# Prompt attention taken two heads at a time, each head on its own half of the TensorE array

## The chip, the cores and the metric

The kernel is one program on one core of one Trainium2 chip. The metric is the device time of one execution in microseconds (us). Before the change three timed runs gave 1269.4, 1271.23 and 1272.8 us: a median of 1271.23 us. One further execution was profiled; that one took 1273.75 us, of which the profile covers a span of 1272.0 us.

Engines are named as the profile names them: PE is the matrix engine (TensorE), PEld its weight loads, DVE VectorE, ACT ScalarE, POOL GpSimd, SP the engine that issues most DMAs.

## The reference, cut to what matters

One inference step of a decoder layer on 256 prompt rows and 32 sample rows: normalise, one wide input projection, a short convolution branch, an attention branch, gates and an output projection, then a retrieval layer (PEER). The change touches the prompt's attention alone. It has three groups of 8 heads of width 64, each group with its own window and dilation; the softmaxes of the three groups of a head are joined.

```python
N_SLOTS, HEAD_DIM, Q_BLOCK = 8, 64, 128
GROUPS = ((128, 1), (512, 4), (2048, 16))
def _dilated_group(q, k_ext, v_ext, ...):          # one group, all 8 heads
    s = einsum('bthd,btkhd->bthk', q, kg)
    s = s * (HEAD_DIM ** -0.5) - slopes[:, None] * dist[None, :]
    s = where(valid, s, -inf)
    m = max(s); p = exp(s - m); l = sum(p)
    o = einsum('bthk,btkhd->bthd', p, vg) / l
    lse = m + log(l)
def _combine(outs, lses):                          # over the three groups
    w = softmax(stack(lses, axis=0), axis=0)
    return sum(w[..., None] * stack(outs, axis=0), axis=0)
```

Because the groups of a head are joined by their denominators, the kernel takes one softmax over the scores of the three groups side by side, and adds the three groups' values into one output.

## The kernel before, in words

**Weights stream past the whole kernel.** 368 blocks of 128 x 1024 floats are loaded in a fixed order (`load_to`, four raw buffers), and each is split into two fp32r halves: ACT makes `whi` (L102), DVE or POOL `wlo` (L103), up to three blocks ahead. A projection block is 8 times 3 matmuls (`mm3`, L118 to L120) into one of two PSUM banks called `acc`. The order of the blocks is: 12 for q, 12 for k, 12 for v, 24 for the convolution, 16 for its output and gate A, 12 for attention's output and gate B, 8 for W_o, 16 for PEER's queries, 128 + 128 for its experts.

**Everything else of attention is threaded between these blocks.** Each piece of attention is a Python generator in a list (`Flow`). `flow.step()` is called at the start and in the middle of most projection blocks; it lets each generator in the list emit its next piece of instructions. A generator may hand back a condition (free PSUM banks, free buffers), and then waits whole steps until it holds. There are six PSUM banks called `bg` for this work. So the order of instructions on every engine is fixed when the program is built: a piece of attention that PE has to do stands between two projection matmuls, and PE takes its queue in order.

**Prompt attention before** (`attn_prompt(t, s)`): t is a tile of 128 queries (0 or 1; keys are 128 (t+1)), s one of 8 heads. 16 generators, in turn:

- scores (L307): for each of three groups a matmul with 64 rows of contraction (the head's 64 channels, in rows 0 to 63 for an even head and 64 to 127 for an odd one), 128 query columns and 128 or 256 keys. Every fp32 matmul is two PE instructions, so a head has 6 on PE;
- bias and mask on DVE (L312, for tile 1 also L315), the softmax (`softmax`, L286 to L292: maximum and scale on DVE, a step; exp on ACT, a step; reciprocal and multiply on DVE, a step);
- transposes of the probabilities on PE (L328), 3 for tile 0, 6 for tile 1, into banks of four; ACT copies them to SBUF (L332);
- values (L338): 3 or 6 matmuls with 128 rows and 64 columns of stationary data (V of the head), accumulated in 64 partitions of one bank: 6 or 12 PE instructions;
- DVE copies the 64 x 128 result to `oT` (L342).

**Sample attention** runs through the same list: scores at L372 and L381, values at L426 and L434, transposes at L408 and L444. Its matmuls have 32 columns of stationary data, and four of them in a row go to four column groups of the array. Each of its 28 chunks of keys or values is loaded by POOL's queue when a buffer comes free.

What follows attention is `split_o`, which needs all heads, and the first block that reads its result stands at block 76. `flow.drain()` ahead of that block empties the list.

Of the kernel before, what the change touches and what calls it, by code (L numbers as in the profile page):

```python
# [10 lines left out]
F32 = mybir.dt.float32  # L11
# [5 lines left out]
OP = mybir.AluOpType  # L17
AX = mybir.AxisListType

P = 128  # L20
D = 1024
NT = 288
# [4 lines left out]
HD = 64  # L27
# [39 lines left out]
def emit(ctx, tc, a):  # L67
# [127 lines left out]
    if True:  # L195
        with ExitStack() as c1:
# [44 lines left out]
            sc_t = Banks(wk, "sc", 3)  # L241
            pt_t = Banks(wk, "pt", 2)
# [52 lines left out]
            def attn_prompt(t, s):  # L295
                pr, hf = divmod(s, 2)
                rows = slice(64 * hf, 64 * hf + 64)
# [4 lines left out]
                yield lambda: bg.free >= (nk if vdone[0] else nk + 1) and sc_t.free >= 1  # L302
                sc_t.free -= 1
                pb = [bg.get() for _ in range(nk)]
# [5 lines left out]
                sc = wk.tile([P, 1024], F32, tag="sc", name=f"sc{t}_{s}", bufs=sc_t.n)  # L310
                n1 = n if t == 0 else 512
                V.scalar_tensor_tensor(sc[:, :n1], biasP[:, off:off + n1], -8.0 * SLOPES[s], pb[0][:, :n1],  # L312
                                       op0=OP.mult, op1=OP.add)
                if t:
                    V.scalar_tensor_tensor(sc[:, 512:768], biasP[:, off + 512:off + 768], -8.0 * SLOPES[s],  # L315
                                           pb[1][:, :256], op0=OP.mult, op1=OP.add)
                bg.put(nk, later=True)
                yield from softmax(sc, n, f"pp{t}_{s}")
                yield lambda: bg.free >= nk and pt_t.free >= 1 and vdone[0]
                pt_t.free -= 1  # L320
                pt = wk.tile([P, 8, P], F32, tag="pt", name=f"pt{t}_{s}", bufs=pt_t.n)
                tbs = []
                for j0 in range(0, nb, 4):
                    j1 = min(nb, j0 + 4)
                    tb = bg.get()
                    tbs.append((tb, j0, j1))
                    for j in range(j0, j1):
                        T.transpose(tb[:, (j - j0) * P:(j - j0 + 1) * P], sc[:, j * P:(j + 1) * P], ident)  # L328
                sc_t.put(1, later=True)
                yield  # L330
                for tb, j0, j1 in tbs:
                    S.copy(pt[:, j0:j1, :].rearrange("p a b -> p (a b)"), tb[:, :(j1 - j0) * P])  # L332
                    bg.put(1, later=True)
                yield lambda: bg.free >= 1 and vdone[0]
                o = bg.get()
                for j in range(nb):
                    g, kb = divmod(j, nk)
                    T.matmul(o[rows, :P], vn[:, kb, g * 512 + s * HD:g * 512 + (s + 1) * HD], pt[:, j, :],  # L338
                             start=j == 0, stop=j == nb - 1)
                pt_t.put(1, later=True)  # L340
                yield
# [956 lines left out]
```

## Time and profile before

| what | value |
|---|---|
| median of 3 timed runs | 1271.23 us |
| the profiled execution | 1273.75 us |
| its span in the profile | 1272.0 us |
| PE busy over the span | 1233.2 us, 97% |
| DVE / ACT / POOL busy | 938.8 / 592.4 / 147.2 us |
| mean granted TensorE clock | 0.991 |
| prompt attention on PE, first to last instruction | 105 to 316 us of the span |

A row of the page's fifth part names a line, an engine, an operation, the tiles written and read, how often it ran, its busy time with the mean of one, and the idle time before it with what ended it. The PE durations are those of single instructions that overlap: two matmuls that start 0.13 us apart are each shown with 0.3 us. So what a stretch of PE work costs is read from starts, that is from the distance between the projection matmul ahead of it and the one behind it, and not from the sum of durations. The chain of waits shows stretches in this way: each piece lasts until the next begins.

### The profile page before, as it was taken

The page shows a single profiled execution, that of the slowest core. Times are in us where ns is not written, and L with a number is a line of the kernel's source. Part 1 is how long each engine was busy: PE and PEld are TensorE (multiplying, and loading weights), DVE is VectorE, ACT ScalarE, POOL GpSimd, SP SyncE. Part 2 cuts the span into 40 slices and gives each one's busy share as a digit, 9 for nine tenths or more (in the row PEclk, how much of TensorE's full clock was granted, in tenths as well). Part 3 has the DMA queues.
Part 4 walks back from the last instruction along what each step waited for, and adds up shares of the span by engine and source line. Part 5 has one row for each costly group of instructions (what it writes and reads, how often), then busy time and mean ns, then how long its engine had stood idle before and what let it go on. Part 6 is the DMA issues. An engine that isn't in the chain of part 4 may idle for free.

```text
span 1272.0 us, 23011 instructions
## 1 busy us (share of the span) xinstructions
PE 1233.2 (97%) x9140; PEld 1129.3 (89%) x9140; DVE 938.8 (74%) x1732; ACT 592.4 (47%) x978; POOL 147.2 (12%) x107
## 2 busy tenths in 40 slices
PE   9999999999998899999999999999999999999996
PEld 9898998888998899989999999999888888888884
DVE  6836376764555566998997898999677777777875
ACT  5334443333353455534554444444455555555553
POOL 1000000000000033444400000000111111111100
PEclk9999999999998899999999999999999999999998
DMA  8687666666458667768677777666778888888872
GB/s 326 223 292 262 239 236 224 214 233 224 146 166 282 234 235 274 273 241 287 243 257 263 286 260 280 248 225 219 273 256 301 305 308 297 309 303 296 311 253 102
DMA packets 67900, 324.49 MB, mean 255 GB/s; under 512 B 8512, under 2 KB 8672, under 8 KB 58832
## 3 DMA queue, kind: packets, MB, share of 16 engines
q1 hardware_dynamic: 55984, 249.46, 56.1%
q0 software_dynamic: 9600, 67.19, 14.1%
q10 hardware_dynamic: 2208, 6.37, 1.3%
q8 instruction: 72, 1.18, 0.4%
q14 instruction: 36, 0.29, 0.1%
HBM read 317.01 MB, written 60.10 MB: 296 GB/s over the span
## 4 chain that ended last, share of the span: by engine, by line
PE 86%; DVE 7%; ACT 2%; DMA 2%; issue 2%; SPq 1%; DVEq 0%; ACTq 0%
PE wide L1080 26%; PE acc L118 17%; PE acc L119 16%; PE acc L120 16%; PE wide L1000 2%; DVE wlo L103 2%; DMA raw<-wpack 2%; PE bg L338 1%; ACT whi L102 1%; PE bg L307 1%; PE bg L426 1%; PE bg L372 1%; DVE tp_eq L851 1%; PE bg L328 1%; DVE qbd L358 1%
## 5 line engine op out<-in xcount | busy, mean ns | idle before, releaser
L103 DVE TENSOR_TENSOR wlo<-raw,whi 128x1024 fp32r<-128x1024 f32 x338 | 417.5, 1236 | 243.0 <-ACT whi L102 240.9
L102 ACT CAST whi<-raw 128x1024 fp32r<-128x1024 f32 x368 | 386.3, 1050 | 181.6 <-PE wide L1080 158.5
L118 PE MATMUL acc<-h2H,whi 128*128 128x256 f32 x1024 | 292.4, 286 | 0.0
L120 PE MATMUL acc<-h2H,wlo 128*128 128x256 f32 x1024 | 287.7, 281 | 4.3 <-DVE wlo L103 4.0
L119 PE MATMUL acc<-h2L,whi 128*128 128x256 f32 x1024 | 289.5, 283 | 0.0
L1080 PE MATMUL wide<-whi,aa 128*128 128x512 f32 x1008 | 270.0, 389 | 1.6 <-ACT aa L1067 1.6
L1080 PEld LDWEIGHTS wide<-whi,aa 128*128 128x128 f32 x1008 | 189.1, 188 | 41.8 <-ACT aa L1067 2.7
L120 PEld LDWEIGHTS acc<-h2H,wlo 128*128 128x128 f32 x1024 | 192.5, 188 | 4.9 <-DVE wlo L103 4.5
L118 PEld LDWEIGHTS acc<-h2H,whi 128*128 128x128 f32 x1024 | 194.0, 190 | 0.2 <-issue 0.2
L119 PEld LDWEIGHTS acc<-h2L,whi 128*128 128x128 f32 x1024 | 193.6, 189 | 0.0
L118 PE MATMUL acc<-hH,whi 128*128 128x288 f32 x512 | 157.3, 307 | 1.8 <-ACT hH L478 1.1
L1080 PE MATMUL wide<-wlo,aa 128*128 128x512 f32 x504 | 155.1, 389 | 0.0
L120 PE MATMUL acc<-hH,wlo 128*128 128x288 f32 x512 | 150.7, 294 | 1.5 <-DVE wlo L103 1.5
L119 PE MATMUL acc<-hL,whi 128*128 128x288 f32 x512 | 151.2, 295 | 0.4 <-DVE hL L480 0.4
L1080 PEld LDWEIGHTS wide<-wlo,aa 128*128 128x128 f32 x504 | 94.6, 188 | 19.6
L118 PEld LDWEIGHTS acc<-hH,whi 128*128 128x128 f32 x512 | 96.0, 188 | 13.5 <-issue 8.5
L120 PEld LDWEIGHTS acc<-hH,wlo 128*128 128x128 f32 x512 | 96.3, 188 | 1.8 <-DVE wlo L103 1.8
L119 PEld LDWEIGHTS acc<-hL,whi 128*128 128x128 f32 x512 | 96.2, 188 | 0.6 <-DVE hL L480 0.6
L103 POOL TENSOR_TENSOR wlo<-raw,whi 128x1024 fp32r<-128x1024 f32 x30 | 76.1, 2537 | 130.8 <-ACT whi L102 123.4
L952 ACT ACTIVATE act<-acc 128x256 f32<-128x256 f32 (+30 forms) x124 | 40.8, 329 | 95.2 <-PE acc L120 94.9
L1091 POOL DMA_INDIRECT gt<-uv,eidx x32 | 48.6, 1517 | 271.0 <-DVE accS L1100 258.1
L949 ACT ACTIVATE hots<-acc 128x256 f32<-128x256 f32 (+31 forms) x65 | 18.5, 284 | 121.1 <-issue 115.7
(319 smaller groups left out, 1669.4 us busy)
## 6 DMA issues: line engine op xcount, KB each, us to landing
raw<-wpack SPq DMA_DIRECT2D x368, 512.0 KB, 3.8
kvs<-cache SPq DMA_DIRECT2D x32, 1020.0 KB, 6.9
kvs<-cache SPq DMA_DIRECT2D x16, 1016.0 KB, 7.3
kv<-kc POOLq DMA_DIRECT2D x14, 1024.0 KB, 6.8
kv<-vc POOLq DMA_DIRECT2D x14, 1024.0 KB, 6.0
kvs<-cache SPq DMA_DIRECT2D x8, 496.0 KB, 4.8
kT_out<-kT ACTq DMA_DIRECT2D x1, 1728.0 KB
v_out<-vn ACTq DMA_DIRECT2D x6, 256.0 KB, 5.5
```

What stands on the lines that cost most here:

```text
L102: S.copy(hi, raw)
L103: (G if i in pool_lo else V).tensor_sub(lo, raw, hi.bitcast(F32))
L118: T.matmul(out, wh, xh, start=first, stop=False)
L119: T.matmul(out, wh, xl, start=False, stop=False)
L120: T.matmul(out, wl, xh, start=False, stop=last)
L307: T.matmul(dst, qT[rows, g * 4 + pr, t * P:(t + 1) * P], kT[rows, g * 4 + pr, 0:w], start=True, stop=True)
L328: T.transpose(tb[:, (j - j0) * P:(j - j0 + 1) * P], sc[:, j * P:(j + 1) * P], ident)
L949: S.activation(e[:, :g], o[:, :g], AF.Gelu)
L952: S.activation(dst[:, g:], o[:, g:NP], AF.Gelu)
L1000: T.matmul(full[:, jj * P:(jj + 1) * P], e[:, 1, j // 2, :, j % 2], w[:, i, j // 2, :, j % 2], start=i == 0, stop=i == 1)
L1080: T.matmul(vacc[t][:, nn], x[:, tt], w[:, nn], start=i == 0 and j == 0, stop=i == 127 and j == 2)
L1091: G.indirect_dma_start(out=gt, out_offset=None, in_=a["uv"], in_offset=bass.IndirectOffsetOnAxis(ap=eidx[:, j:j + 1], axis=0))
```

## The change

`attn_prompt(t, pr)` now takes a pair of heads, 2 pr and 2 pr + 1. There are 8 generators in place of 16.

- Scores: for each group one matmul of the even head (rows 0 to 63) and one of the odd head (rows 64 to 127) by turns, each head into a bank of its own. For tile 1 the first two groups are one step, the third a later one, with two more banks.
- The softmaxes of both heads go side by side in the same steps.
- Transposes come three at a time for each head: one round for tile 0, two rounds for tile 1. After each round and its copies on ACT come the value matmuls of those three blocks, the two heads by turns, into partitions 0 to 63 and 64 to 127 of one bank.
- One DVE copy of 128 x 128 moves both heads' result.
- Four score buffers of 992 columns in place of three of 1024, and four steps in place of two between the starts of generators.

The number of matmuls, transposes, copies on ACT and bias operations stays the same; the copies to `oT` are 8 in place of 16.

```diff
-            sc_t = Banks(wk, "sc", 3)
+            sc_t = Banks(wk, "sc", 4)
...
-            def attn_prompt(t, s):
+            def attn_prompt(t, pr):
+                heads = (2 * pr, 2 * pr + 1)
+                rows = (slice(0, 64), slice(64, 128))
...
-                for g in range(3):
-                    dst = pb[0][:, g * w:(g + 1) * w] if t == 0 or g < 2 else pb[1][:, :w]
-                    T.matmul(dst, qT[rows, g * 4 + pr, t * P:(t + 1) * P], kT[rows, g * 4 + pr, 0:w],
-                             start=True, stop=True)
+                for gs in (range(3),) if t == 0 else (range(2), range(2, 3)):
+                    if gs.start:
+                        yield lambda: bg.free >= (2 if vdone[0] else 3)
+                    pb = [bg.get() for _ in range(2)]
+                    for g in gs:
+                        for h in range(2):
+                            T.matmul(pb[h][:, (g - gs.start) * w:(g - gs.start + 1) * w],
+                                     qT[rows[h], g * 4 + pr, t * P:(t + 1) * P], kT[rows[h], g * 4 + pr, 0:w],
+                                     start=True, stop=True)
+                    yield
...
+                sm = [softmax(scs[h], n, f"pp{t}_{heads[h]}") for h in range(2)]
+                while True:
+                    if [next(x, 1) for x in sm] == [1, 1]:
+                        break
+                    yield
...
+                for j0 in range(0, nb, 3):
...
+                    for h in range(2):
+                        tb = bg.get()
+                        tbs.append(tb)
+                        for j in range(3):
+                            T.transpose(tb[:, j * P:(j + 1) * P], scs[h][:, (j0 + j) * P:(j0 + j + 1) * P], ident)
...
+                    yield
+                    for h in range(2):
+                        S.copy(pt[:, 4 * h:4 * h + 3, :].rearrange("p a b -> p (a b)"), tbs[h][:, :3 * P])
+                    bg.put(2, later=True)
+                    yield
+                    for j in range(j0, j0 + 3):
+                        g, kb = divmod(j, nk)
+                        for h in range(2):
+                            T.matmul(o[rows[h], :P], vn[:, kb, g * 512 + heads[h] * HD:g * 512 + (heads[h] + 1) * HD],
+                                     pt[:, 4 * h + j - j0, :], start=j == 0, stop=j == nb - 1)
...
-                V.tensor_copy(oT[rows, pr, t * P:(t + 1) * P], o[rows, :P])
-                punits[0] += 1
+                V.tensor_copy(oT[:, pr, t * P:(t + 1) * P], o[:, :P])
+                punits[0] += 2
```

The built programs show what this does to the order. On PE, around the convolution's last blocks, before: the values of head 2 (L338) and the scores of head 5 (L307) of tile 1 stand in one gap between projection matmuls (L118 to L120).

```order
L338 MATMUL bg71_3151<-pt1_2_3102,vn_91 64x128 x6
L307 MATMUL bg72_3165<-kT_90,qT_89 128x256 x2
L307 MATMUL bg73_3166<-kT_90,qT_89 128x256
L118 MATMUL acc56_3176<-hH_81,whi58_3032 128x288
L119 MATMUL acc56_3176<-hL_209,whi58_3032 128x288
L120 MATMUL acc56_3176<-hH_81,wlo58_3033 128x288
```

The same place in the changed program, where the scores are L311, the transposes L335 and the values L348: the scores of heads 4 and 5 alternate between two banks (bg65, bg66), and their third group comes in a later gap, next to the second round of transposes of heads 2 and 3 (sc1_2, sc1_3).

```order
L120 MATMUL acc56_3118<-hH_81,wlo58_3001 128x288
L311 MATMUL bg65_3178<-kT_90,qT_89 128x256
L311 MATMUL bg66_3179<-kT_90,qT_89 128x256
L311 MATMUL bg65_3178<-kT_90,qT_89 128x256
L311 MATMUL bg66_3179<-kT_90,qT_89 128x256
L118 MATMUL acc57_3190<-hH_81,whi59_3064 128x288
...
L335 MATMUL bg67_3239<-ident_70,sc1_2_2776 128x128 x3
L335 MATMUL bg68_3243<-ident_70,sc1_3_2777 128x128 x3
L311 MATMUL bg69_3247<-kT_90,qT_89 128x256
L311 MATMUL bg70_3248<-kT_90,qT_89 128x256
L118 MATMUL acc58_3257<-zH_1825,whi60_3112 128x288
```

What moved: 3 + 3 score matmuls of two heads in two gaps became 4 + 2 in two gaps, each by turns over the two row halves. In all, prompt attention stands on PE in 36 places in place of 48 (12 of transposes, 12 of values, 12 of scores, where before there were 16 of each); some of these share a gap with each other or with sample attention. The last values of the prompt stand in block 67, before in block 64 or 65; the sample's last work stands in block 69 as before.

On DVE, the softmax of heads 4 and 5 of tile 1 before: each head's bias (L312, L315), maximum (L286) and scale (L287) are a run of their own, with a weight split (L103) between the heads.

```order
L312 SCALAR_TENSOR_TENSOR sc1_4_3158<-bias_77,bg69_3132 128x512
L315 SCALAR_TENSOR_TENSOR sc1_4_3158<-bias_77,bg70_3133 128x256
L286 TENSOR_REDUCE pp1_4_m_3161<-sc1_4_3158 128x1
L287 TENSOR_SCALAR pp1_4_m_3161<-pp1_4_m_3161 128x1
L103 TENSOR_TENSOR wlo60_3171<-raw60_2942,whi60_3170 128x1024
L342 COPY oT_93<-bg71_3151 64x128
L312 SCALAR_TENSOR_TENSOR sc1_5_3206<-bias_77,bg72_3165 128x512
L315 SCALAR_TENSOR_TENSOR sc1_5_3206<-bias_77,bg73_3166 128x256
L286 TENSOR_REDUCE pp1_5_m_3209<-sc1_5_3206 128x1
L287 TENSOR_SCALAR pp1_5_m_3209<-pp1_5_m_3209 128x1
```

In the changed program (bias is L317, the copy to `oT` L352) both heads' operations stand together:

```order
L317 SCALAR_TENSOR_TENSOR sc1_4_3176<-bias_77,bg69_3247 128x256
L317 SCALAR_TENSOR_TENSOR sc1_5_3177<-bias_77,bg70_3248 128x256
L286 TENSOR_REDUCE pp1_4_m_3280<-sc1_4_3176 128x1
L287 TENSOR_SCALAR pp1_4_m_3280<-pp1_4_m_3280 128x1
L286 TENSOR_REDUCE pp1_5_m_3284<-sc1_5_3177 128x1
L287 TENSOR_SCALAR pp1_5_m_3284<-pp1_5_m_3284 128x1
L103 TENSOR_TENSOR wlo63_3318<-raw63_3068,whi63_3317 128x1024
L352 COPY oT_93<-bg64_3155 128x128
L291 RECIPROCAL pp1_4_l_3281<-pp1_4_l_3281 128x1
L292 TENSOR_SCALAR sc1_4_3176<-sc1_4_3176,pp1_4_l_3281 128x768
L291 RECIPROCAL pp1_5_l_3285<-pp1_5_l_3285 128x1
L292 TENSOR_SCALAR sc1_5_3177<-sc1_5_3177,pp1_5_l_3285 128x768
```

What moved: runs of DVE work twice as long, half as often, and both heads' maximum behind both heads' last bias.

## Rows read from the trace of the kernel before

**Rows 1.** The page's first part: busy time, share of the span, instructions of each engine.
```profile
PE 1233.2 (97%) x9140; PEld 1129.3 (89%) x9140; DVE 938.8 (74%) x1732; ACT 592.4 (47%) x978; POOL 147.2 (12%) x107
```

**Rows 2.** Busy time by stretch (start:end length, engines), granted clock, DMA share, GB/s.
```profile
150.00:320.00 170.00, 170.00 (x1366) 145.06 (x1364) 106.64 (x258) 68.12 (x120) 7.92 (x15) 1.00 0.64 222
...
391.00:428.00 37.00, 29.91 (x198) 28.87 (x197) 18.06 (x31) 12.83 (x22) 1.59 (x3) 0.91 0.82 286
428.00:480.00 52.00, 49.76 (x357) 49.16 (x358) 32.69 (x103) 28.34 (x46) 12.29 (x6) 0.93 0.66 229
```

**Rows 3.** PE's prompt attention groups, shapes apart: line, tiles, count, busy us, mean ns.
```profile
L338 PE MATMUL bg<-pt,vn 128*64 128x128 f32 x144 | 18.6, 278 | 0.0
...
L307 PE MATMUL bg<-kT,qT 64*128 64x256 f32 x48 | 12.5, 393 | 0.0
...
L307 PE MATMUL bg<-kT,qT 64*128 64x128 f32 x48 | 6.9, 289 | 0.0
```

**Rows 4.** PE in order of time around one head's scores: start us, us, instruction.
```profile
108.94 0.29 PE L118 MATMUL acc<-hH,whi 128*128 128x288 f32 x1
109.07 0.29 PE L119 MATMUL acc<-hL,whi 128*128 128x288 f32 x1
109.21 0.29 PE L120 MATMUL acc<-hH,wlo 128*128 128x288 f32 x1
109.43 0.93 PE L307 MATMUL bg<-kT,qT 64*128 64x128 f32 x6
110.29 0.40 PE L118 MATMUL acc<-hH,whi 128*128 128x288 f32 x1
110.53 0.30 PE L119 MATMUL acc<-hL,whi 128*128 128x288 f32 x1
```

**Rows 5.** The chain of waits, single pieces: start us, us, what, instructions.
```profile
180.36 0.86 PE bg L307 x6
...
199.47 0.80 PE bg L338 x6
...
239.15 1.49 PE bg L307 x6
...
284.24 0.66 PE bg L328 x6
...
290.77 1.46 PE bg L338 x12
```

**Rows 6.** The chain of waits: four column groups, then two heads in a row.
```profile
164.97 1.01 PE bg L372 x32
165.98 1.19 PE bg L307 x12
...
169.92 1.07 PE bg L338 x12
```

**Rows 7.** DVE's prompt attention groups from 100 to 345 us.
```profile
L286 DVE TENSOR_REDUCE pp_m<-sc 128x1 f32<-128x768 f32 x8 | 7.6, 953 | 0.3
L312 DVE SCALAR_TENSOR_TENSOR sc<-bias,bg 128x512 f32<-128x512 f32 x8 | 5.4, 681 | 0.1
...
L292 DVE TENSOR_SCALAR sc<-sc,pp_l 128x768 f32<-128x768 f32 x8 | 5.0, 621 | 0.3
L342 DVE COPY oT<-bg 64x128 f32<-64x128 f32 x16 | 4.6, 285 | 0.9 <-PE bg L338 0.7
...
L315 DVE SCALAR_TENSOR_TENSOR sc<-bias,bg 128x256 f32<-128x256 f32 x8 | 3.3, 412 | 0.0
```

**Rows 8.** In order of time: one head's exp, its last softmax step, its transposes.
```profile
270.89 0.94 ACT L289 ACTIVATE sc<-sc,pp_m 128x768 f32<-128x768 f32 x1
...
278.38 0.62 DVE L292 TENSOR_SCALAR sc<-sc,pp_l 128x768 f32<-128x768 f32 x1
...
284.08 0.82 PE L328 MATMUL bg<-ident,sc 128*128 128x128 f32 x6
```

**Rows 9.** PE's longest wait behind the attention stretch, from the timeline.
```profile
407.29 0.58 PE L118 MATMUL acc<-mixH,whi 128*128 128x288 f32 x1 [5.66 <-DVE x2T L723]
```

More of the change, by code (lines that the diff above doesn't have):

```diff
@@ L309, in attn_prompt @@
-                yield
[L310 to L339, printed above, removed]
@@ L340, in attn_prompt @@
-                pt_t.put(1, later=True)
-                yield
-                V.tensor_copy(oT[rows, pr, t * P:(t + 1) * P], o[rows, :P])
-                punits[0] += 1
+                yield lambda: bg.free >= (2 if vdone[0] else 3) and sc_t.free >= 2
+                sc_t.free -= 2
+                scs = [wk.tile([P, 992], F32, tag="sc", name=f"sc{t}_{heads[h]}", bufs=sc_t.n) for h in range(2)]
+                for gs in (range(3),) if t == 0 else (range(2), range(2, 3)):
[8 more added lines that the diff above has]
+                    yield
+                    c0, c1 = gs.start * w, gs.stop * w
+                    for h in range(2):
+                        V.scalar_tensor_tensor(scs[h][:, c0:c1], biasP[:, off + c0:off + c1], -8.0 * SLOPES[heads[h]],
+                                               pb[h][:, :c1 - c0], op0=OP.mult, op1=OP.add)
+                    bg.put(2, later=True)
@@ new lines, in attn_prompt @@
+                sm = [softmax(scs[h], n, f"pp{t}_{heads[h]}") for h in range(2)]
[3 more added lines that the diff above has]
+                    yield
+                o = None
+                for j0 in range(0, nb, 3):
+                    yield lambda: bg.free >= (3 if o is None else 2) and pt_t.free >= 1 and vdone[0]
+                    pt_t.free -= 1
+                    pt = wk.tile([P, 8, P], F32, tag="pt", name=f"pt{t}_{pr}_{j0}", bufs=pt_t.n)
+                    tbs = []
+                    for h in range(2):
[3 more added lines that the diff above has]
+                            T.transpose(tb[:, j * P:(j + 1) * P], scs[h][:, (j0 + j) * P:(j0 + j + 1) * P], ident)
+                    if o is None:
+                        o = bg.get()
+                    if j0 + 3 == nb:
+                        sc_t.put(2, later=True)
+                    yield
+                    for h in range(2):
+                        S.copy(pt[:, 4 * h:4 * h + 3, :].rearrange("p a b -> p (a b)"), tbs[h][:, :3 * P])
+                    bg.put(2, later=True)
+                    yield
+                    for j in range(j0, j0 + 3):
+                        g, kb = divmod(j, nk)
+                        for h in range(2):
+                            T.matmul(o[rows[h], :P], vn[:, kb, g * 512 + heads[h] * HD:g * 512 + (heads[h] + 1) * HD],
+                                     pt[:, 4 * h + j - j0, :], start=j == 0, stop=j == nb - 1)
+                    pt_t.put(1, later=True)
@@ L392, in sample_rest @@
                 pb = sps[st]
-                sc = wk.tile([P, 1024], F32, tag="sc", name=f"scS{st}", bufs=sc_t.n)
+                sc = wk.tile([P, 992], F32, tag="sc", name=f"scS{st}", bufs=sc_t.n)
                 V.tensor_add(sc[:, 0:512], pb[0], biasS[:, 0:512])
@@ L437, in sample_rest @@
                 sc_t.free -= 1
-                on = wk.tile([P, 1024], F32, tag="sc", name=f"on{st}", bufs=sc_t.n)
+                on = wk.tile([P, 992], F32, tag="sc", name=f"on{st}", bufs=sc_t.n)
                 V.tensor_copy(on[:, :512], o)
```

11 lines of the change are left out of this document (4 added, 7 removed).

## The prediction

> **What bounds the kernel now.** I read the page's first part first: PE is busy 97% of the span, DVE 74%, nothing else over half [rows 1]. An average says little about one stage, so the table by stretches comes next. Prompt attention runs from 105 to 316 us. There PE is busy without a gap (170.00 of 170.00 us from 150 to 320), at the full granted clock (1.00, that is 2.4 GHz), while DVE has 106.64 us and the DMA engines 64% [rows 2]. The reader is to see that in this stage every microsecond of PE's queue is a microsecond of the end, and that nothing else is near full. Behind it lie two stretches that are not like that: from 391 to 428 PE is busy only 29.91 of 37 us and the granted clock falls to a mean of 0.91; from 428 to 480 it is 0.93 [rows 2].
>
> The groups of PE's instructions name attention's share, but their sums can't be used: 18.6 us for the values and 12.5 + 6.9 us for the scores count overlapping instructions in full [rows 3]. So I go to the timeline and the chain of waits and read distances between starts.
>
> **What one visit to attention costs on PE.** Neighbouring projection matmuls start 0.13 us apart (108.94, 109.07, 109.21). Around one head's scores of tile 0 the starts go on with 109.43, 110.29 and 110.53 [rows 4]: from the last projection matmul ahead to the second behind are 1.32 us where 2 x 0.13 would do, so the visit costs 1.06 us. Of these 0.86 us are the piece itself [rows 5], and 0.19 us are going in (0.22 in place of 0.13) and coming out (0.24 in place of 0.13). When two pieces of divided-array work stand side by side, the 0.19 is paid once. Transposes use the whole array; other gaps of theirs show no such extra, and 6 take 0.66 us, 0.11 each [rows 5].
>
> The pieces [rows 5]: scores of a head 0.86 us in tile 0 and 1.49 in tile 1, values 0.80 and 1.46, transposes 0.33 and 0.66. From 6 to 12 value instructions 0.66 us are added: 0.11 per instruction, and about 0.14 to start. With 256 keys a score instruction takes (1.49 - 0.86) / 6 = 0.105 us more than with 128, so 0.216.
>
> **Before, summed.** In tile 0 two heads of the eight happened to stand back to back twice, once in scores (12 instructions in 1.19 us) and once in values (12 in 1.07 us) [rows 6]. Scores of tile 0: 6 x 0.86 + 1.19 = 6.35. Scores of tile 1: 8 x 1.49 = 11.9. Values of tile 0: 6 x 0.80 + 1.07 = 5.9; of tile 1: 8 x 1.46 = 11.7. Transposes 72 x 0.11 = 7.9. Of the visits with divided arrays 20 stand without another beside them: 20 x 0.19 = 3.8. Sum 47.5 us.
>
> **Do two halves of the array overlap?** The same two back-to-back pieces answer it. They are two heads, an even one and an odd one. Had they run one behind the other, six more instructions at 0.11 would give 0.86 + 0.66 = 1.52 us for scores and 0.80 + 0.66 = 1.46 for values. They took 1.19 and 1.07, so the second head added 0.33 and 0.27: it ran in its own half while the first still had about half its instructions to go [rows 6]. Sample attention shows it in the steady state: 32 instructions over four column groups in 1.01 us, 0.032 each, a quarter and a bit of 0.11 [rows 6]. The change puts the heads by turns, so the second can start behind the first two instructions of the first (one fp32 matmul).
>
> I take that a pair's piece is one head's piece plus a late start of 0.10 us, about one instruction. Bounds: nothing from below (the four column groups start within a few hundredths), and from above the 0.33 and 0.27 seen. I choose 0.10 because the order by turns removes the cause of the long offset, the five or six instructions of the first head that stood ahead.
>
> At one place the Trainium skill says something else. By "TensorE: Matmul & The Clock Gate", section "The mechanism", a weight load runs beside a matmul in flight only when the two use different row groups. Two value matmuls use all rows, so by that rule the halves by columns would gain little. This trace speaks against it: the 32 instructions in 1.01 us all use 128 rows [rows 6]. I keep the consequence as a rival, with its price from rows.
>
> **After, summed.** Scores of tile 0: 4 x (0.86 + 0.10) = 3.8. Scores of tile 1 come in two visits, of four instructions a head, 1.49 - 2 x 0.216 + 0.10 = 1.16, and of two, 1.49 - 4 x 0.216 + 0.10 = 0.73: 4 x 1.89 = 7.6. Values: 12 visits (4 in tile 0, 8 in tile 1, since tile 1's are cut in two rounds) of 0.80 + 0.10: 10.8. Transposes 72 x 0.11 = 7.9, unchanged. Visits with divided arrays that stand alone, counted in the new order: 15 x 0.19 = 2.9. Sum 33.0 us. PE saves 47.5 - 33.0 = 14.5 us. With a late start of nothing the saving is 14.5 + 24 x 0.10 = 16.9; with 0.33 and 0.27 it is 14.5 - 12 x 0.23 - 12 x 0.17 = 9.7 us.
>
> **What is not PE's own.** The copies to `oT` are halved, 8 x 0.285 = 2.3 us less DVE [rows 7], worth nothing where PE is full. ACT's copies keep their number within one and so cost nothing. The buffers of 992 columns hold the same 768 or 992 numbers. The weight stream has to come faster: 222 GB/s over 170 us become 243 over 155; the stretch from 391 shows 286 GB/s [rows 2]. POOL's key and value loads wait for sample matmuls that stand in the same blocks as before, and come earlier with them.
>
> What PE may newly wait for is the softmax. Both heads must now be done before either is transposed. From a pair's last scores in tile 1 on, DVE has 2 x (0.41 + 0.95 + 0.62) = 3.96 us to do, a single head had 0.68 + 0.41 + 0.95 + 0.62 = 2.66 [rows 7], and ACT a second exp of 0.94 [rows 8]: the way is 2.2 us longer. Behind a waiting transpose stand PE's projection matmuls, so such a wait is paid in full. The cover: a head whose last softmax step ended at 278.38 + 0.62 = 279.00 was transposed at 284.08, 5.1 us later [rows 8]. Four of the eight pairs keep before's distance of 2.5 weight blocks from last scores to first transposes, the others have more. Bounds: 0 where the slack covers it, and 4 x 2.2 = 8.8 where it is gone at all four. I take 1.5 us, nearer to the row.
>
> **The time.** 14.5 - 1.5 = 13 us. The profiled execution took 1273.75 us, so it would take 1260.7. It stands 2.5 us above the median of the timed runs, which becomes 1271.2 - 13 = 1258.
>
> **Rivals.**
>
> 1. *Halves by columns do not overlap, halves by rows do.* Then 12 value visits take 1.46 in place of 0.90: 6.7 us of the saving go, 1258 + 6.7 = 1265. For it: only the skill's rule; against it: 1.07 us for 12 and 1.01 us for 32 [rows 6]. Chance 0.04.
> 2. *The change does not do what it says: by turns, the halves do not overlap at all.* Pieces of pairs are then serial: scores 4 x 1.52 + 4 x (1.06 + 0.86) + 4 x (0.63 + 0.43) = 18.0, values 12 x 1.46 = 17.5, and 7.9 + 2.9: 46.3 us, 1.2 less than before; with the 1.5 us of waits 1271.5. Against it the same rows. Chance 0.03.
> 3. *The gain is made and partly given back behind attention.* At 407 PE has waited 5.66 us [rows 9], and around such waits the clock falls: 0.09 x 37 = 3.3 us lost in one stretch, 0.07 x 52 = 3.6 in the other [rows 2]. If one more such fall comes, or a wait there grows because data comes no earlier, 3 to 6 us go: 1261 to 1264. For it: these stretches hang on a copy burst and not on PE. Against it: the burst is issued in the order of the weight blocks, so it moves with PE. Chance 0.09. The other way, one fall less would give 1255.
> 4. *Slower: the double softmax stalls PE.* DVE takes its queue in order, and its doubled runs (two of 0.41 and two of 0.95 us in a row, 2.7 us without the small ones between) delay both the transposes and the reads that free `acc` banks. To lose 3.8 us net, the eight pairs must cost 18.3 us, 2.3 us each: each set of transposes comes 5.1 + 2.3 = 7.4 us later against PE than now. Above 1.8 us a pair the change is no gain. With 3 us each the time is 1271 - 14.5 + 24 = 1281. For it: DVE is busy 63% here, and both softmaxes are in one run. Against it: DVE's sum does not grow, and its slack of 5.1 us. Chance 0.04.
>
> **Chances and range.** The forecast has 0.80, the rivals 0.04, 0.03, 0.09 and 0.04. The forecast's own range is 1271 - 16.9 = 1254 to 1271 - 9.7 + 3 = 1264. The range from 1253 to 1266 takes in rivals 1 and 3. A measurement of this kernel tells 0.3%, 3.8 us, from no change: below 1267.4 is faster. The forecast and rivals 1 and 3 are there with small tails (0.90), rival 2 and the tails are the same (0.06), rival 4 is slower (0.04).
>
> **What would show it.** In the changed profile's chain, a pair's scores of tile 0 (12 instructions) as a piece of 0.86 to 1.19 us, 8 and 4 instructions of tile 1 as 1.06 to 1.39 and 0.63 to 0.96; 12 value instructions in 0.80 to 1.07. Values near 1.46 there mean rival 1, scores near 1.52 too mean rival 2. Idle time of PE ahead of L335 ended by DVE's L292 is rival 4's; beyond 2 us in all it proves my 1.5 too small. Attention's last values should start near 308 us in place of 314, though they stand 2.5 blocks later. The stretches from 391 on should look as before but 13 us earlier; if they are longer, it is rival 3. I am wrong in kind if PE shows the short pieces and the end has not moved by at least 9 us.

## The result and the profile after

| | median us | ratio to before, with its 95% interval |
|---|---|---|
| before, 4 runs | 1270.55 | |
| after, 4 runs | 1256.94 (1256.61 to 1258.31) | 0.9893 [0.9876, 0.991] |
| after, repeated later, 4 runs; before there 1271.34 | 1254.86 (1254.14 to 1255.64) | 0.9864 [0.9847, 0.9882] |

The change makes the kernel faster by 13.6 us in the first set and by 16.5 us in the second. The profiled execution after took 1258.31 us with a span of 1256.3 us; the repeated kernel's took 1255.64 us with 1253.6 us.

The first part of the profile's page after the change: busy time, share of the span, instructions of each engine. PE has as many instructions as in [rows 1], in 14.3 us less busy time; DVE has the eight copies fewer that the edit leaves out.

```profile
PE 1218.9 (97%) x9140; PEld 1117.6 (89%) x9140; DVE 935.3 (74%) x1724; ACT 591.0 (47%) x978; POOL 147.3 (12%) x107
```

Busy time by stretch after (columns as in [rows 2]): the inside of attention, then the two stretches behind it. These two are cut 13 us earlier than in [rows 2].

```profile
142.00:307.00 165.00, 165.00 (x1464) 141.81 (x1464) 105.57 (x251) 70.84 (x126) 7.92 (x15) 1.00 0.67 237
...
378.00:415.00 37.00, 29.15 (x192) 28.11 (x190) 17.62 (x29) 13.51 (x23) 2.11 (x4) 0.91 0.79 277
415.00:467.00 52.00, 50.70 (x370) 50.34 (x371) 32.47 (x101) 27.94 (x45) 11.94 (x5) 0.93 0.66 238
```

PE is still busy without a gap at the full clock, with 1464 instructions in 165 us where [rows 2] had 1366 in 170: 8.87 a microsecond in place of 8.04. The DMA engines bring 237 GB/s in place of 222, and are still far from the 286 of [rows 2]. The stretches behind attention have the old shares and the old clock.

PE's attention groups, shapes apart, after (columns as in [rows 3], from 95 to 345 us):

```profile
L348 PE MATMUL bg<-pt,vn 128*64 128x128 f32 x144 | 10.5, 281 | 0.0
L311 PE MATMUL bg<-kT,qT 64*128 64x256 f32 x48 | 7.3, 411 | 0.0
...
L311 PE MATMUL bg<-kT,qT 64*128 64x128 f32 x48 | 3.8, 289 | 0.0
```

The values had 18.6 us in [rows 3] and have 10.5; the scores had 12.5 and 6.9 and have 7.3 and 3.8. A value instruction is as long as before (281 ns against 278) and a score instruction about as long (411 and 289 against 393 and 289): nearly the same instructions now lie over each other.

The timeline of PE around a pair's scores of tile 0 after, which answers to [rows 4]: start, us, instruction.

```profile
194.18 0.29 PE L120 MATMUL acc<-hH,wlo 128*128 128x288 f32 x1
194.40 0.94 PE L311 MATMUL bg<-kT,qT 64*128 64x128 f32 x12
195.27 0.40 PE L118 MATMUL acc<-hH,whi 128*128 128x288 f32 x1
195.50 0.29 PE L119 MATMUL acc<-hL,whi 128*128 128x288 f32 x1
```

Twelve instructions of two heads stand between the same gaps (0.22 in, 0.23 out) for 0.87 us, where six of one head stood for 0.86. Other pieces in the chain of waits, which answer to [rows 5, 6]:

```profile
180.04 0.87 PE bg L311 x12
...
197.12 0.81 PE bg L348 x12
...
207.94 1.06 PE bg L311 x8
...
214.39 0.63 PE bg L311 x4
```

All pieces of a kind agree within 0.01 us. Summed: scores of tile 0, 4 x 0.87 = 3.5; of tile 1, 4 x (1.06 + 0.63) = 6.8; values 12 x 0.81 = 9.7; transposes 72 x 0.11 = 7.9; 15 ways in and out at 0.19 = 2.9. The 15 are the visits with no other divided-array work beside them. That is 30.7 us where 47.5 stood before.

Where the time came from, read from starts of projection matmuls in the timelines. The first of block 24, ahead of attention, and the first of block 92, behind it, before:

```profile
99.69 0.30 PE L118 MATMUL acc<-hH,whi 128*128 128x288 f32 x1
...
413.19 0.38 PE L118 MATMUL acc<-mixH,whi 128*128 128x288 f32 x1
```

and after:

```profile
98.69 0.30 PE L118 MATMUL acc<-hH,whi 128*128 128x288 f32 x1
...
396.03 0.35 PE L118 MATMUL acc<-mixH,whi 128*128 128x288 f32 x1
```

These are 313.5 us before, 297.3 after and 297.1 in the repeated kernel. So the stage gives 16.2 and 16.4 us. About 1 us more lies ahead of block 24 in the profiled executions; the edit changes nothing there.

What PE waited for in the stage after (engine, line, waited for: us, times, longest; from 100 to 345 us):

```profile
PE acc L120 <- DVE qbd L368: 1.9, 1, 1.9
PE acc L118 <- ACT vt L592: 0.7, 1, 0.7
```

No wait stands ahead of the transposes (L335). The last values of the prompt start at 306.80 us in place of 314.09:

```profile
306.80 0.88 PE L348 MATMUL bg<-pt,vn 128*64 128x128 f32 x12
```

And behind attention, from 330 to 470 us, PE's longest wait is the one of [rows 9], as long as it was (5.6 us here, 5.66 there):

```profile
PE acc L118 <- DVE x2T L735: 6.8, 2, 5.6
```

### The profile page after: what moved, and what is told of

It reads as the page before. It is cut to its first block, busy times and chain, and to the rows that moved or that the text cites. A ratio compares the mean times of both kernels' runs of the same rounds, so it can differ in the third digit from the quotient of the medians.

```text
span 1256.3 us, 23010 instructions
## 1 busy us (share of the span) xinstructions
PE 1218.9 (97%) x9140; PEld 1117.6 (89%) x9140; DVE 935.3 (74%) x1724; ACT 591.0 (47%) x978; POOL 147.3 (12%) x107
## 3 DMA queue, kind: packets, MB, share of 16 engines
q8 instruction: 71, 1.16, 0.4%
## 4 chain that ended last, share of the span: by engine, by line
PE 87%; DVE 6%; ACT 2%; DMA 2%; issue 1%; SPq 0%; DVEq 0%; ACTq 0%
PE wide L1092 27%; PE acc L118 17%; PE acc L119 16%; PE acc L120 16%; PE wide L1012 2%; DVE wlo L103 2%; DMA raw<-wpack 2%; ACT whi L102 1%; PE bg L436 1%; PE bg L382 1%; DVE tp_eq L863 1%; PE bg L348 1%; PE bg L311 1%; PE bg L335 1%; PE bg L226 1%
## 5 line engine op out<-in xcount | busy, mean ns | idle before, releaser
L103 DVE TENSOR_TENSOR wlo<-raw,whi 128x1024 fp32r<-128x1024 f32 x338 | 417.6, 1237 | 245.2 <-ACT whi L102 243.4
L118 PE MATMUL acc<-h2H,whi 128*128 128x256 f32 x1024 | 293.6, 287 | 0.0
L120 PE MATMUL acc<-h2H,wlo 128*128 128x256 f32 x1024 | 289.1, 282 | 4.4 <-DVE wlo L103 4.1
L120 PEld LDWEIGHTS acc<-h2H,wlo 128*128 128x128 f32 x1024 | 193.4, 189 | 5.0 <-DVE wlo L103 4.5
L118 PEld LDWEIGHTS acc<-h2H,whi 128*128 128x128 f32 x1024 | 195.2, 191 | 0.2 <-issue 0.2
L118 PE MATMUL acc<-hH,whi 128*128 128x288 f32 x512 | 157.1, 307 | 1.8 <-ACT hH L488 1.1
L120 PE MATMUL acc<-hH,wlo 128*128 128x288 f32 x512 | 151.4, 296 | 2.1 <-DVE qbd L368 1.9
L118 PEld LDWEIGHTS acc<-hH,whi 128*128 128x128 f32 x512 | 96.6, 189 | 15.3 <-issue 10.5
L120 PEld LDWEIGHTS acc<-hH,wlo 128*128 128x128 f32 x512 | 96.8, 189 | 0.4 <-DVE wlo L103 0.4
L103 POOL TENSOR_TENSOR wlo<-raw,whi 128x1024 fp32r<-128x1024 f32 x30 | 76.1, 2536 | 131.5 <-ACT whi L102 119.4
L961 ACT ACTIVATE hots<-acc 128x256 f32<-128x256 f32 (+31 forms) x65 | 18.4, 284 | 122.1 <-issue 114.3
```

The costliest lines, as they stand in the source:

```text
L103: (G if i in pool_lo else V).tensor_sub(lo, raw, hi.bitcast(F32))
L118: T.matmul(out, wh, xh, start=first, stop=False)
L120: T.matmul(out, wl, xh, start=False, stop=last)
L961: S.activation(e[:, :g], o[:, :g], AF.Gelu)
```

## The experiments

Each edit is to the changed kernel, but for `before_twice`. "Stage" is the time from the first projection matmul of block 24 to that of block 92 in the profiled execution, as above. again, by_head, same_half and one_visit share one set of runs of the kernel before (median 1271.34); max_twice, max_five, fewest and by_two another (1271.35); the last four a third (1271.7).

**again**: the changed kernel, with no edit.

> The changed kernel once more, beside more runs of the one before. Theory: PE's visits to attention save about 17 us by block 92 and about 1 us is lost again further on by falls of the clock that differ from execution to execution, so the median is 1256 to 1258 and the difference from before 13 to 16 us. Rival: the first four runs fell low by chance and the difference is the full 17 us (1254). Either way the distance from the first projection matmul to block 92 is 17 us shorter than before.

Measured: 1254.86 us, 0.9864 [0.9847, 0.9882], stage 297.1 us, pieces as above to 0.01 us. The two sets differ by 2 us in the median. Between the two profiled executions 2.6 us appear behind attention, in blocks 96 to 99. The later of the two stretches there, in the repeated kernel:

```profile
415.00:467.00 52.00, 50.52 (x387) 50.15 (x388) 34.30 (x113) 30.31 (x48) 11.95 (x5) 1.00 0.73 252
```

It runs at 1.00 here and at 0.93 above: the first execution had a second fall to the half clock (1.2 GHz), 6.8 us long from 416.6, and this one had none there. The kernel before had both falls in its profile, at 406.5 and 433.8. The fall comes or stays away from execution to execution of one and the same kernel, so about 2.6 us of scatter go with it, which is nothing that the change gives back. It is enough for the 2 us between the medians, though only the profiled executions show where a fall was.

**by_head**: the same visits, but each head's matmuls in a row.

```diff
-                    for g in gs:
-                        for h in range(2):
+                    for h in range(2):
+                        for g in gs:
...
-                    for j in range(j0, j0 + 3):
-                        g, kb = divmod(j, nk)
-                        for h in range(2):
+                    for h in range(2):
+                        for j in range(j0, j0 + 3):
+                            g, kb = divmod(j, nk)
```

> Pairs as in the changed kernel, but inside a visit all matmuls of the even head stand ahead of all of the odd head. Theory (order by turns removes the late start): tile 0's scores take 1.19 us a visit in place of 0.87, tile 1's eight instructions 1.28 to 1.39 in place of 1.06, its four unchanged at 0.63 (one matmul a head is by turns anyway), values 1.07 in place of 0.81: 1.3 + 1.1 + 3.1 = 5.5 us slower than the changed kernel, about 1262. Rival (two halves overlap whatever the order): pieces as in the changed kernel, 1257. Rival (without turns nothing overlaps): pieces 1.52, 1.92 and 1.46, about 1271.

Measured: 1259.58 us, 0.99 [0.9882, 0.9918], 4.7 us above the repeated kernel; stage 301.0, 3.9 longer. Its pieces in the chain of waits:

```profile
181.26 1.19 PE bg L311 x12
...
210.34 1.07 PE bg L311 x8
214.20 1.07 PE bg L348 x12
```

The pieces of twelve cost what two heads in a row cost in [rows 6], 1.19 and 1.07: 4 x 0.32 + 12 x 0.26 = 4.4 us, which accounts for the difference (4.7 in the medians, 3.9 in the stage). The miss is the piece of eight, four instructions a head: it takes 1.07 here and 1.06 by turns, with no late start. The single starts in the trace say the same. In a score piece of twelve the second head's first instruction starts 0.33 us behind the first head's (196.54 against 196.21), just behind the third of its six; in a piece of eight it starts 0.01 us behind (210.286 against 210.272).

**by_two**: two matmuls of one head, two of the other, then the third of each, so four instructions of one head stand ahead of the other's first.

```diff
-                    for g in gs:
-                        for h in range(2):
+                    for g, h in [(g, h) for g0 in range(gs.start, gs.stop, 2) for h in range(2)
+                                 for g in range(g0, min(g0 + 2, gs.stop))]:
...
+                    for j, h in [(j, h) for j1 in (j0, j0 + 2) for h in range(2)
+                                 for j in range(j1, min(j1 + 2, j0 + 3))]:
```

> Inside a visit two matmuls (four PE instructions) of the even head, two of the odd, then the last of each. Theory A (the second half starts at once as long as no more than four instructions of the other half stand ahead of it, as the visits of eight score instructions showed when taken head by head): pieces as in the changed kernel, 0.87 and 0.81, time 1255. Theory B (every instruction ahead delays the other half, 0.33 us for six): about 0.2 us more in 4 score and 12 value visits, 3 us slower.

Measured: 1255.44 us, 0.9871 [0.985, 0.9892], the time of the repeated kernel. Its chain:

```profile
180.34 0.88 PE bg L311 x12
...
184.00 0.81 PE bg L348 x12
...
208.27 1.07 PE bg L311 x8
```

Behind four instructions of the other half nothing starts late. The strict turns of the change are not needed; it is enough that no more than four of one head stand first.

**same_half**: the pairs are two even or two odd heads. The pieces, softmaxes and buffers are those of the change, but both heads lie in one half of the rows and, for values, of the columns (with a bank and a copy to `oT` for each head, and so four free banks to wait for where the change waits for three).

```diff
-                heads = (2 * pr, 2 * pr + 1)
-                rows = (slice(0, 64), slice(64, 128))
+                hf = pr % 2
+                heads = (4 * (pr // 2) + hf, 4 * (pr // 2) + 2 + hf)
+                rows = (slice(64 * hf, 64 * hf + 64),) * 2
...
```

> Pairs of heads of the same parity (0 with 2, 1 with 3), so both heads of a visit use the same half of the array; the two results go to two banks and are copied by two DVE instructions. Theory (the gain is the overlap of two halves): scores 1.52 us in tile 0, 1.92 and 1.06 in tile 1, values 1.46 to 1.47, so 4 x 0.65 + 4 x 0.86 + 4 x 0.43 + 12 x 0.65 = 15.6 us of the gain go: 1272, as before the change. Rival (the gain comes from fewer visits and bigger pieces): it stays below 1262.

Measured: 1268.78 us over 11 runs, 0.9976 [0.9967, 0.9985]; stage 312.7 us. Its chain (scores L312, values L349):

```profile
187.82 1.46 PE bg L349 x12
189.27 1.53 PE bg L312 x12
...
223.46 1.92 PE bg L312 x8
...
230.82 1.06 PE bg L312 x4
```

These are two heads one behind the other. Their places move too, presumably because of the fourth bank (the last values start at 331.68 us in place of 306.80), and more of them stand side by side: 8 ways in and out in place of 15. Summed: 4 x (1.53 + 1.92 + 1.06) + 12 x 1.46 + 7.9 + 8 x 0.19 = 45.0 us on PE, 14.3 more than with two halves, and the stage is 15.6 us longer than the repeated kernel's. The clock fell to the lower level for 3.4 us at 120.6 in this stage and not in the repeated kernel's, worth up to 1.7. Against the kernel before 2.6 us remain in the median, which fits PE's 47.5 - 45.0 = 2.5, most of it ways saved; the profiled stage shows 0.8, that fall included. So of the 16.5 us about 14 hang on the halves, and the rest on fewer ways in and out.

**one_visit**: all scores of a pair in tile 1 in one visit, with four banks.

```diff
-                for gs in (range(3),) if t == 0 else (range(2), range(2, 3)):
-                    if gs.start:
-                        yield lambda: bg.free >= (2 if vdone[0] else 3)
-                    pb = [bg.get() for _ in range(2)]
+                parts = (range(3),) if t == 0 else (range(2), range(2, 3))
+                pbs = [[bg.get() for _ in range(2)] for _ in parts]
+                for gs, pb in zip(parts, pbs):
...
```

> Tile 1's scores of a pair in one visit of 12 instructions (four banks) in place of two of 8 and 4. Theory (a visit costs 0.19 us of way in and out and 0.20 of its own start): 4 x 0.39 = 1.6 us less on PE, more where the visit now stands next to the values: 1255 to 1256. Rival (the softmax's run on DVE gets longer, its slack ahead of the transposes is used up): PE waits ahead of the transposes and the time is 1257 to 1260.

Measured: 1254.92 us, 0.9869 [0.9851, 0.9887]; stage 295.6, 1.5 less than the repeated kernel's, yet the same median. Its chain has the joined piece, 0.19 us shorter than 1.06 + 0.63:

```profile
211.29 1.50 PE bg L310 x12
```

A gain of 1 to 2 us is within what these runs scatter; whether it is there stays open.

**max_twice** and **max_five**: the prompt's maxima are taken two or five times over, which adds 8 x 0.55 + 8 x 0.94 = 12 us (or 48 us) of DVE work to the softmaxes and changes no value. Nothing else in the program changes. The edit of max_twice; max_five has a 5 for the 2.

```diff
-                V.reduce_max(m, t[:, :n], axis=AX.X)
+                for _ in range(2 if name.startswith("pp") else 1):
+                    V.reduce_max(m, t[:, :n], axis=AX.X)
```

> The changed kernel with the maximum of each prompt head taken twice on DVE (the second gives the same number): 2 x 0.55 us more in a pair of tile 0, 2 x 0.95 in tile 1. In the changed kernel's trace the last softmax step of the second head ends 0.6, 0.75 and 0.9 us ahead of the transposes in three pairs of tile 0, 2.5 and 5.0 in two of tile 1, over 15 in the others. Theory (the double softmax has used up the slack, so DVE decides next): PE waits ahead of those three transposes, 1.1 less each slack, about 1 us in all: 1256. Rival (DVE is far from deciding): no waits, 1255.

> The same with the maximum taken five times: 4.4 us more DVE work in a pair of tile 0, 7.6 in tile 1. Theory (slack as read): waits ahead of the transposes of 3.8 + 3.6 + 3.5 us in tile 0 and 5.1 + 2.6 in tile 1, at most 19 us, less where DVE makes up between pairs: 1265 to 1273. Rival (the weight splits and the freeing of banks behind DVE's longer runs stall PE first, in many places): over 1273. Rival (DVE's idle third takes it): under 1260.

Measured: max_twice 1260.87 us, 0.9918 [0.9904, 0.9932], stage 302.2, 5.2 us longer than the repeated kernel's; max_five 1303.0 us, 1.0237 [1.022, 1.0255], stage 345.1, 48 us longer. Waits of PE from 100 to 345 us, first with two:

```profile
PE acc L118 <- ACT vt L593: 2.7, 1, 2.7
PE bg L336 <- DVE pp_l L292: 1.2, 2, 0.7
PE acc L120 <- DVE qbd L364: 1.2, 1, 1.2
PE acc L118 <- DVE cy L630: 0.6, 1, 0.6
```

and with five, the four longest:

```profile
PE bg L336 <- DVE pp_l L292: 12.3, 4, 3.7
PE acc L118 <- DVE cy L630: 6.0, 1, 6.0
PE acc L118 <- DVE es L616: 4.7, 1, 4.7
PE acc L118 <- ACT vt L593: 3.9, 1, 3.9
...
```

With two, PE waits ahead of the transposes (L336 here) for the softmax for the first time. One of these places, in the timeline of max_twice: a pair's last softmax step, and the transposes behind it.

```profile
195.63 0.42 DVE L293 TENSOR_SCALAR sc<-sc,pp_l 128x384 f32<-128x384 f32 x1
...
195.67 0.52 PE L336 MATMUL bg<-ident,sc 128*128 128x128 f32 x3 [0.71 <-DVE pp_l L292]
```

In the changed kernel itself such a place has a little room; in its timeline:

```profile
204.23 0.42 DVE L292 TENSOR_SCALAR sc<-sc,pp_l 128x384 f32<-128x384 f32 x1
...
205.54 0.82 PE L335 MATMUL bg<-ident,sc 128*128 128x128 f32 x6
```

From the end at 204.65 to 205.54 are 0.9 us. Three pairs of tile 0 have 0.6, 0.75 and 0.9 us, two of tile 1 have 2.5 and 5.0. Before, a head of tile 1 had 5.1 [rows 8]; in tile 0 head 2 had 3.1 and heads 4 to 7 had 5.3 to 6.0. Head 4, for one, ended at 188.43:

```profile
188.01 0.42 DVE L292 TENSOR_SCALAR sc<-sc,pp_l 128x384 f32<-128x384 f32 x1
...
193.74 0.49 PE L328 MATMUL bg<-ident,sc 128*128 128x128 f32 x3
```

So the slack is largely used up in tile 0, and the mechanism of rival 4 is real, though small at 12 us of added work. Of the 5.2 us that max_twice's stage lost, 3.0 are waits of PE (5.7 against the repeated kernel's 2.7), 1.2 of them ahead of the transposes and the rest where `acc` banks come free late (`vt`, `cy`). One fall of the clock, for 3.4 us at 119.8 behind the wait for `vt`, is worth up to 1.7 more. DVE work that the forecast took for hidden thus costs about 5 us of 12, where I had expected about 1. Of max_five's 48 us the waits and the clock have about half each (last section), so it is by chance that they equal the 48 us of added work.

**before_twice**: the same edit with two maxima, in the kernel before.

> The kernel before the change with the maximum of each prompt head taken twice: the same 12 us of DVE work as in max_twice, which cost the changed kernel 6.0 us. Theory (the change used up DVE's slack; the kernel before has 5 us from a head's last softmax step to its transposes): 0 to 1.5 us slower, 1271 to 1273. Rival (DVE's work in this stage is half on the path in either kernel): about 6 us slower, 1277.

Measured over 11 runs: 1274.83 us, 1.0023 [1.0014, 1.0032], so 1.8 to 4.1 us slower; stage 314.6, 1.1 us longer than before. The same 12 us of DVE work cost the kernel before about 1 us of its stage and the changed one about 5, of which the clock may have up to 1.7. In the medians the difference is less sure: 3.1 us here, and for max_twice 6.0 against the repeated set but 3.1 against the first, each taken by its gain over the kernel before (16.5 - 10.5 and 13.6 - 10.5). That falls between the two theories. What sets the kernels apart clearly is the wait ahead of the prompt's transposes, 1.2 us in max_twice and none here. That DVE's time has become dearer in the changed kernel is likely from that, and not settled by the medians.

**fewest**: one_visit, and tile 1's values in one visit of 24 instructions, from one buffer that holds both rounds' transposes.

```diff
-            pt_t = Banks(wk, "pt", 2)
+            pt_t, pq_t = Banks(wk, "pt", 1), Banks(wk, "pq", 1)
...
+                pt = wk.tile([P, 12, P], F32, tag="pq", name=f"pt{t}_{pr}", bufs=pq_t.n)
...
+                for j in range(nb):
+                    g, kb = divmod(j, nk)
+                    for h in range(2):
+                        T.matmul(o[rows[h], :P], vn[:, kb, g * 512 + heads[h] * HD:g * 512 + (heads[h] + 1) * HD],
+                                 pt[:, 6 * h + j, :], start=j == 0, stop=j == nb - 1)
...
```

> Scores of tile 1 in one visit of 12 instructions and values of tile 1 in one visit of 24, one wider buffer for the transposed probabilities of the prompt and one for the sample's. Theory (a visit costs 0.19 for the way and 0.14 to 0.20 for its start): 4 x 0.20 + 4 x 0.15 less in pieces and about eight ways less, 2.9 us less on PE than in the changed kernel: b92 about 393 us into the span in place of 396, time 1252 to 1253. Rival (what PE saves here is not seen in the time, as with the one visit for scores): 1255.

Measured: 1258.23 us, 0.9895 [0.988, 0.991]; stage 300.3, 3.2 longer than the repeated kernel's. The piece is cheap, 24 instructions for the price of 12 in one half:

```profile
229.89 1.46 PE bg L348 x24
```

But its waits in the stage grew:

```profile
PE acc L118 <- ACT zH L631: 1.8, 1, 1.8
PE acc L120 <- DVE qbd L368: 1.8, 1, 1.8
PE bg L336 <- DVE sc L292: 1.3, 2, 1.1
PE acc L118 <- DVE es L615: 0.7, 1, 0.7
```

They are 5.6 us in place of 2.7, and 1.3 of them stand ahead of the transposes, where the changed kernel has none. I read these 1.3 as DVE being late, since pairs follow each other more closely here. The waits are not all: the clock fell twice in this stage, for 3.4 us each, at 108.1 and at 278.8, in the repeated kernel not at all between 58 and 389 us. The second fall lies just behind the wait of 1.8 us for `zH`:

```profile
276.00:286.00 10.00, 8.08 (x60) 7.29 (x60) 5.17 (x13) 4.42 (x9) 0.00 (x0) 0.83 0.90 340
```

PE's pieces are 1.4 us shorter and 8 ways in and out fewer, 2.9 us less; the waits are 2.9 more, and the two falls lose up to 1.7 each: 3.4 us longer, where 3.2 were measured. So less work on PE made the kernel no faster here, because its waits grew as much and the clock fell besides. The fall at 108.1 follows a wait that the changed kernel has too (1.8 us there, without a fall), so part of the loss may be scatter.

**norm_act**, **one_act** and **fewest_act**: the last softmax step goes from DVE to ACT, in the changed kernel, in one_visit and in fewest.

```diff
-                V.tensor_scalar_mul(t[:, :n], t[:, :n], l)
+                S.activation(t[:, :n], t[:, :n], AF.Copy, scale=l)
```

> The changed kernel with the softmax's last multiply (16 of 0.42 to 0.62 us for the prompt, 2 of 0.74 for the sample) on ACT in place of DVE. Theory (DVE has next to no slack left and waits of PE are still there, 3 us in the stage): 0 to 2 us faster, 1253 to 1255. Rival (ACT's queue then delays weight halves and copies): 1 to 3 us slower.

> Tile 1's scores in one visit, and the softmax's last multiply on ACT. Theory: one visit's 1.9 us at block 92 stays, no new waits: 1253 to 1254. Rival: as one_visit, 1255.

> Scores and values of tile 1 in one visit each, and the softmax's last multiply on ACT. Theory (fewest lost 3 us because its heads come closer together and DVE is late, 1.8 + 1.3 + 0.7 us of waits on ACT and DVE): with 10 us less on DVE the waits go and PE's shorter pieces show: b92 393 to 395, time 1252 to 1254. Rival (ACT is the late one there): 1257 or more.

Measured: 1259.21 us, 0.9895 [0.988, 0.9911]; 1259.34 us, 0.99 [0.9885, 0.9914]; 1259.25 us, 0.9902 [0.9887, 0.9918]. Their stages are 300.8, 300.1 and 300.1 us: 3.7 and 4.5 longer than the repeated kernel's and one_visit's, and as long as that of fewest. The waits of norm_act:

```profile
PE acc L118 <- ACT vt L592: 2.3, 1, 2.3
PE acc L120 <- DVE qbd L368: 1.8, 1, 1.8
PE bg L348 <- ACT pt L342: 0.7, 2, 0.4
```

Now ACT is late, in the copies ahead of the values (`pt`, L342) and in `vt`. These waits are 2.1 us above the repeated kernel's; the rest of the 3.7 us is not accounted for. The stages of one_act and fewest_act have a fall of the clock for 3.4 us at 108.0, that of fewest_act one more at 248.0. So moving this step to ACT gave nothing back, and fewest_act does not bear out that DVE alone held fewest up. None of the versions beats the changed kernel by more than the scatter; one_visit and by_two equal it.

## Why the prediction was right

**The time.** 1258 was forecast and 1256.94 measured, 13.6 us less than before against a forecast of 13; the repeated set has 16.5. That the first set lies within 1 us of the forecast is partly luck, since the stage itself gave 16. The mechanism is the one forecast: same_half, with the same pieces and the same softmaxes but without two halves, is only 2.6 us faster than before.

**The late start was mis-sized.** The forecast charged 0.10 us for it in 24 visits. Measured is 0.01 in the pieces of twelve (0.87 against 0.86, 0.81 against 0.80), and the tile 1 pieces take 1.06 and 0.63, which are 1.16 and 0.73 less 0.10. PE's sum is 30.7 and not 33.0; the saving is 16.8 us, the bound of 16.9 that I had given for a late start of nothing. The two pieces of [rows 6] showed the right cause, five or six instructions of one head ahead, and by_head reproduces their 0.32 and 0.26. I then chose a value near the lower end because it was "about one instruction", with no row for it; the four column groups in [rows 6] were the nearer row.

**The waits were mis-sized the other way.** I took 1.5 us for the double softmax. The view of waits has 2.6 us in the stage against 2.2 before, and the stage saves 16.2 to 16.4 where PE's sum saves 16.8: about 0.5 us, none of it ahead of L335. My reason, 5.1 us of slack, was read from a head of tile 1 [rows 8]; heads 4 to 7 of tile 0 had as much before, and three of tile 0's pairs have only 0.6 to 0.9 us left. I had counted one way in which the cover shrinks, the 2.2 us that a pair's softmax is longer. The timelines show two. From the scores to the end of the last softmax step the two pairs of heads 4 to 7 take 10.3 and 11.3 us, where the single heads took 7.3 to 9.1. And from the scores to the transposes they have 11.1 and 12.1 us, where the single heads had 13.3 to 15.0: the distance counted in weight blocks is kept, but the blocks pass sooner, presumably because there is less attention work between them. That no pair waited was decided by less than a microsecond, which is in part luck.

The two errors in size, 2.3 and 1.0 us, are both on the cautious side and make up the distance from 13 to the stage's 16.2 and 16.4. In the first profiled execution 1.5 us of the stage's gain and of the lead ahead of it were lost behind attention (block 92 starts 17.2 us earlier, the span is 15.7 us shorter), in the repeated one nothing (17.1 and 18.4).

**Rival 1 and rival 2** fall by single pieces. The Trainium skill says in "TensorE: Matmul & The Clock Gate", section "The mechanism", that a weight load runs beside a matmul in flight only when the two use different row groups. These runs do not agree: value matmuls of 128 rows and 64 columns take 0.81 us for twelve by turns over the two column halves, and 1.46 in one half (same_half). The pieces that rival 2 gave for serial halves (1.52, 1.92, 1.06 and 1.46 us) are those that same_half measures.

**Rival 3** was put as something that the change may bring. The falls of the clock behind attention are in [rows 2] too; one of them comes or goes from execution to execution, with 2.6 us, and the longest wait there stays 5.6 us. So it adds scatter to the gain and is no effect of the change.

**Rival 4** did not happen, but its mechanism is there: with 12 us more on DVE the transposes wait for the last softmax step, and with 48 us the kernel is slower than before. I had put its turning point at 1.8 us a pair: max_twice pays 0.6 (5 / 8) and max_five 6 (48 / 8), in both cases with the clock's part. What the forecast judged wrong is how soon a pair begins to pay: it took DVE, busy 63%, for far from full.

**The rest** came as forecast: the weight stream rose to 237 GB/s and PE's waits in the stage name no weights, and the last values start at 306.80 against 308 forecast. That the copies to `oT` are worth nothing by themselves was not tested.

## What to carry to other kernels

Where two independent small matmuls use opposite row halves or opposite column halves, issue them close to each other: here the second half's work then cost 0.01 us a piece, and turns of one or two matmuls were equally good. Price such a piece from the best overlap that the trace shows, not from a middle between ends. When the bound engine's work is joined into fewer, larger pieces, read the slack of its feeders at the tightest place and not at one example: an engine that is busy two thirds of the time can still be the next to be waited for, and making the bound engine's work still shorter (fewest) gave nothing here. The slack shrinks from both sides, because the bound engine also comes sooner.

## What was not expected of the hardware

The late start of the second half is not in proportion to what stands ahead of it: 0.26 to 0.32 us behind six instructions (by_head), and about 0.01 behind four (by_two, and by_head's piece of eight) or two. In by_head's trace the seventh instruction of a score piece starts at 196.540 us, just behind the third (196.534), and in the piece of eight the fifth at 210.286, just behind the first (210.272). Both would follow if PE reached four instructions ahead; this is an estimate from these starts, and no run tried five. So PE does not take its queue strictly in order, as was said of the kernel before: this matmul of the second head starts ahead of the first head's fourth, fifth and sixth (196.646, 196.757 and 196.869 us).

Waits of PE in this stage came with a fall of the clock. Busy time by stretch over attention, first of the kernel with five maxima:

```profile
105.00:355.00 250.00, 218.12 (x1809) 190.43 (x1807) 175.24 (x367) 87.64 (x152) 9.49 (x18) 0.90 0.56 197
```

and of the repeated kernel:

```profile
105.00:355.00 250.00, 247.32 (x2180) 219.81 (x2177) 153.39 (x342) 109.08 (x187) 9.49 (x18) 1.00 0.63 227
```

PE idles 29 us more, and the clock, 1.00 without the waits, is 0.90 in the mean: it stood at the lower level (1.2 GHz) nine times in this stretch, 48 us in all, and each time PE had waited just before or was waiting. At 0.90 the 250 us lose up to 25 us, nearly as much again as the waits, though part of it falls into the waits: the stage is 48 us longer, and not 54.
